# First projection with the activations held in TensorE: halves of 512 columns, x*C by tokens and then turned, and seven-product groups there and in the output projection

## Chip, cores and metric

The kernel runs on one core of a Trainium2 chip, as one program in one launch. The metric is the device time of that program in microseconds (us). The kernel before took 2130.61 us (median of 3 runs, 2130.58 to 2131.43).

## What is computed

A two-layer decoder trunk on 256 tokens (T) of width 2048 (D), all in float32. Only the first sub-layer is touched by the change:

```python
def short_conv_mixer(u, w_in, conv_w, w_out):
    proj = u @ w_in                                   # 256 x 2048 @ 2048 x 6144
    xin, gate_c, gate_b = jnp.split(proj, 3, axis=-1)
    v = gate_c * xin
    S = v.shape[1]
    vp = jnp.pad(v, ((0, 0), (CONV_WIDTH - 1, 0), (0, 0)))
    conv = sum(conv_w[k] * vp[:, k:k + S] for k in range(CONV_WIDTH))
    return (gate_b * conv) @ w_out                    # 256 x 2048 @ 2048 x 2048
...
h = h + rmsnorm(short_conv_mixer(rmsnorm(h, mix_pre_g[0]), ...), mix_post_g[0])
```

Behind it come a squared-ReLU MLP (2048 to 8192 and back), one shared K/V projection, a stick-breaking attention with its own query and output projections, and a second such MLP. The gain of each norm in front of a projection is multiplied into the operand; the 1/rms of a token may be applied later, since it is one number for each token.

## The kernel before

**Products.** A float32 product is made of three matmuls in the round format `fp32r`: each operand is split into a high part (ScalarE, a copy into `fp32r`: `split`, the `h...` tiles) and a low part (VectorE, raw minus high: `lower`, the `l...` tiles), and high·high, high·low and low·high are added up in PSUM. Weights come from memory in chunks of 512 KB (128 rows x 1024 columns, `chunk`), six raw pages deep.

**Two ways to hold operands.** In every projection but the first, a `Group` (16 chunks of K=128 rows, 1024 columns) holds the activations in TensorE (128 x 128: one K-chunk, one block of 128 tokens) and moves 512 weight columns past them; its output lies by tokens, in four PSUM banks `acc[b][c]` (token block b, column half c). Three such matmuls on one `acc` are one product (`product`, line 563). In the first projection (`convolution`) it is the other way round: a weight tile of 128 x 128 is held, and the 512 columns [high | low] of all 256 tokens move past it (`mms`, part 0), then the low weight tile with the 256 high columns (part 1), both recorded at line 437. The output lies by features, one bank for each of 48 column tiles, 16 K-chunks each. Six tiles are led in together (`lead`, `LEAD = 6`), K-chunk by K-chunk as the weights arrive; the other 42 follow one after another.

**Between the projections.** `combined` adds the two halves of the moved columns, `conv_tile` forms x*C, scales it by 1/rms squared, does the three taps along the tokens (shifts along the free dimension, so by features is the right layout), multiplies by B and 1/rms, and splits the result into the four tiles `y` that the output projection holds. `statistics` gets 1/rms of all tokens as a row by one matmul with ones.

**Seven products.** In most MLP groups some pairs of K-chunks (`seven`, `UP_SEVEN`, `DN_SEVEN`) do the 2 x 2 blocks (two K-chunks, two token blocks, two column halves) by seven products in place of eight, in the manner of Strassen and Winograd: VectorE adds and subtracts weight halves (four operations of 512 columns, `Group.seven`), the activation sums `XS` are formed ahead (`make_forms`), and four products of the seven go into banks of their own, `q5 q6 q1 q7`, which are the four banks that the group before has just left (`next_set`, `qset`). `combine` and `finals` add them into the outputs on VectorE. A group with seven-product pairs (`mixed`) starts with one ordinary pair, and its second pair is already a seven.

**What sets the order.** Every instruction is a task of `Plan`, which lists tasks engine by engine by estimated times and due times; side tasks of TensorE (transposes) are put into its queue where their inputs are expected. Each engine then runs its list strictly in that order. Pages are slots of fixed classes (`SLOTS`): `x4` 8, `c2` 12, `x8` 8.

Lines that the prediction uses: 390 ScalarE activations, 398 VectorE `tensor_tensor`, 405 VectorE `scalar_tensor_tensor`, 437 first projection's matmuls, 444 transposes (`tr`), 563 `product`.

Of the kernel before, what the change touches and what calls it, by code (L numbers as in the profile page):

```python
# [20 lines left out]
LEAD = 6  # L21
# [7 lines left out]
SLOTS = {"raw": 6, "rt": 2, "r2": 2, "hi": 6, "lo": 5, "x8": 8, "x4": 8, "c2": 12}  # L29
# [5 lines left out]
IN_N = [j * KD + i for i in range(KD) for j in range(3)]  # L35
IN_ORDER = [(k, n) for k in range(KD) for n in IN_N[:LEAD]] + [(k, n) for n in IN_N[LEAD:] for k in range(KD)]

# [49 lines left out]
class Plan:  # L87
# [77 lines left out]
    def place(self):  # L165
# [52 lines left out]
        while done < len(tasks):  # L218
# [39 lines left out]
            if e in ("SP", "POOL") and t.kb:  # L258
                issue = 0.06 if e == "SP" else 1.2
# [65 lines left out]
def trunk(ctx, tc, x, xT, vecs, rows, ws, hs, out):  # L325
# [202 lines left out]
    def form(XS, j, i, f):  # L528
        o = (i * 4 + FORM[f]) * P
        return XS[j].view([(o, o + P)], lambda t: t[:, i, FORM[f], :])  # L530

    def make_forms(XS, pairs, r0, r1, name):
# [14 lines left out]
        for j in pairs:  # L547
            XS[j] = page("x4", [P, 2, 4, P], F32R, f"{name}{j}")
            for r, f in ((r0, 0), (r1, 2)):
                src = r.col(j % 2 * 2 * P, (j % 2 + 1) * 2 * P).as3("p (k t) -> p k t", k=2)  # L550
                hi, lw = [
                    XS[j].view([((i * 4 + f) * P, (i * 4 + f + 2) * P)], lambda t, i=i, f=f: t[:, i, f : f + 2, :])
# [16 lines left out]
    class Group:  # L569


        def __init__(self, name, w, base, n, X, banks, evict, ks=1, gains=None, XS=None, sevens=(), seeds=None, qbanks=None, start=None):
            self.name, self.w, self.base, self.n, self.X, self.banks, self.evict = name, w, base, n, X, banks, evict
            self.ks, self.gains, self.XS, self.sevens, self.seeds, self.qbanks = ks, gains, XS, sevens, seeds, qbanks
            self.start = start
# [16 lines left out]
        def parts(self, i):  # L592
            if i not in self.split:
                gains = self.gains(i) if self.gains else None
                self.split[i] = chunk(self.w, self.base + i, f"{self.name}{i}", parts=len(gains) if gains else 1, gains=gains)
# [17 lines left out]
        def seven(self, j, last):  # L613
# [3 lines left out]
            if j in SUMS_BY_DMA:  # L617
                rs = raw_page(f"r{name}s")
                r1 = page("r2", [P, HALF], F32, f"r{name}b")
                twice = w[base + 1][:, HALF:].unsqueeze(1).to_broadcast([P, 2, HALF])  # L620
                load(rs.col().as3("p (a n) -> p a n", a=2), twice, own=(r0, rs))
# [99 lines left out]
        def whole(self):  # L721
# [193 lines left out]
    def convolution():  # L915
        rot = {"i": -1}

        def next_bank(name):
            rot["i"] += 1
            return bank(rot["i"] % 8, name)  # L920

        stores = [page("x4", [P, CW], F32, f"tmp{z}") for z in range(5)]

        def ring(places):
            at = {"i": -1}

            def take():
                at["i"] += 1
                return places[at["i"] % len(places)]
            return take  # L930

        quarter = [stores[z].col(q * T, (q + 1) * T) for z in range(4) for q in range(4)]
        vplaces = [stores[4].col(z * (T + 2), (z + 1) * (T + 2)) for z in range(2)]
        sums, halves, convs, vring = ring(quarter[:8]), ring(quarter[8:11]), ring(quarter[11:13]), ring(vplaces)
        rstd, rstd2 = quarter[13], quarter[14]
        u = [operand(f"u{c}") for c in range(4)]
        acc = page("c2", [P, 2 * T], F32, "sumsq")
        xpair, wsplit = {}, {}
        w = ws["in"]

        def load_x(q):
            if q < KD // 2:
                xpair[q] = page("c2", [P, 2 * T], F32, "x")
                load(xpair[q].col(), xT[:, q * 2 * T : (q + 1) * 2 * T])

        at_tile = {kn: i for i, kn in enumerate(IN_ORDER)}

        def mms(tiles):
            for part in range(2):
                for ps, k, n in tiles:  # L950
                    i = at_tile[k, n]
                    ci = i // CH
                    if ci not in wsplit:
                        wsplit[ci] = chunk(w, ci, f"in{ci}", parts=4 if ci < FIRST else 1)
                    o = i % CH * P
                    wv = wsplit[ci][part].col(o, o + P)
                    xs = u[k // 4].view([(at4(k % 4, 0), at4(k % 4, 0) + 4 * P)], lambda t, k=k: t[:, k % 4].rearrange("p a b t -> p (a b t)"))
                    xh = u[k // 4].view([(at4(k % 4, 0), at4(k % 4, 0) + 2 * P)], lambda t, k=k: t[:, k % 4, 0].rearrange("p b t -> p (b t)"))
                    if part == 0:
                        mm(ps.col(), wv, xs, 0.231, start=k == 0, stop=False)  # L960
                    else:
                        mm(ps.col(0, T), wv, xh, 0.12, start=False, stop=k == KD - 1)

        def combined(ps):
            b = halves()
            act(b, ps.view([(0, 2 * T)], lambda t: t[:, T : 2 * T]), AF.Copy, soon=2.0)
            s = sums()
            tt(s, ps.col(0, T), b, ALU.add, soon=3.0)
            return s

        def enter(k):
            xp, gain = xpair[k // 2].col(k % 2 * T, (k % 2 + 1) * T).as3("p (b t) -> p b t", b=NB), g(G_MIX0, k)
            act(both(u, k, 0), xp, AF.Copy, scale=gain)
            stt(both(u, k, 1), xp, gain, both(u, k, 0), ALU.mult, ALU.subtract)
            if k % 2:
                if k == 1:
                    act(acc.col(), xpair[0].col(), AF.Square, soon=20.0)
                else:
                    sq = page("c2", [P, 2 * T], F32, "sq")
                    act(sq.col(), xpair[k // 2].col(), AF.Square, soon=20.0)  # L980
                    tt(acc.col(), acc.col(), sq.col(), ALU.add, soon=25.0)

        y = [None] * 4
        state = {"scale": False}

        def statistics():
            tt(acc.col(0, T), acc.col(0, T), acc.col(T, 2 * T), ALU.add)
            ps = bank(LEAD - 1, "ms")
            mm(ps.col(0, T), ones.col(), acc.col(0, T), 0.44)
            act(rstd, ps.col(0, T), AF.Sqrt, bias=eps.col(), scale=1.0 / D)  # L990
            recip(rstd)
            tt(rstd2, rstd, rstd, ALU.mult)
            state["scale"] = True

        for o in (0, T + 2):
            v = stores[4].col(o, o + 2)
            plan.task("DVE", 0.1, lambda v=v: nc.vector.memset(v.w(), 0.0), [], [v])

        def conv_tile(i, sx, sc, sb):
            tt(sx, sx, sc, ALU.mult)  # L1000
            v = vring()
            tt(sub(v, 2, T + 2), sx, rstd2, ALU.mult)
            c = convs()
            act(c, sub(v, 2, T + 2), AF.Copy, scale=g(G_C2, i))
# [442 lines left out]
```

## Time and profile before

| | |
|---|---|
| median of three runs | 2130.61 us |
| the profiled execution, its time | 2130.27 us |
| its span | 2128.5 us |
| granted TensorE clock | 0.999 |
| TensorE first matmul | 5.88 us |
| first projection on TensorE | 5.88 to 276.40 us |
| output projection on TensorE | 276.40 to 363.96 us |
| VectorE busy in these two | 194.17 and 45.43 us |

Times inside the profile count from the start of the span. A row of matmuls starts when its first one starts; rows overlap, since a matmul's recorded time includes its way through the array, so the pace of TensorE is read from start to start, not from the mean duration.

### The profile page before, as it was taken

The numbers are of one execution on the slowest core, as the hardware profiler recorded it, in microseconds if no ns is written. First come the engines' busy times: TensorE is split into PE (matmuls) and PEld (weight loads), VectorE is DVE, ScalarE is ACT, GpSimd is POOL, SyncE is SP. The second block draws the span as 40 slices with busy tenths as digits, with TensorE's granted clock in tenths as the row PEclk, the third lists the DMA queues.
The fourth block names the chain that finished last, engine by engine and source line by source line (L and its number), as shares of the span: only waits on it lengthen the run. The fifth ranks groups of instructions, "written<-read, shape, count | busy, mean of one in ns | idle before, by whom it ended". The sixth has DMA issues, their size and how long they took to land.

```text
span 2128.5 us, 28143 instructions
## 1 busy us (share of the span) xinstructions
PE 2111.5 (99%) x9900; PEld 1764.5 (83%) x9900; DVE 1770.7 (83%) x2456; ACT 1307.8 (61%) x1830; POOL 1.0 (0%) x7
## 2 busy tenths in 40 slices
PE   8999999999999999999999999999999999999998
PEld 7888888888888888888888888888888888888886
DVE  7766656899999999999656777558999999999995
ACT  7444445766576576567657776547755765675673
POOL 0000000000000000000000000000000000000000
PEclk9999999999999999999999999999999999999999
DMA  8655576556656755667665455656566566656673
GB/s 288 190 190 189 188 252 199 185 187 218 204 186 198 228 182 195 208 211 248 215 205 168 158 168 170 232 180 220 172 203 227 180 198 208 207 181 208 197 267 127
DMA packets 118653, 427.63 MB, mean 201 GB/s; under 512 B 13168, under 2 KB 13296, under 8 KB 118512
## 3 DMA queue, kind: packets, MB, share of 16 engines
q1 hardware_dynamic: 118368, 425.77, 60.9%
q8 instruction: 77, 1.26, 0.2%
q14 instruction: 64, 0.52, 0.1%
q10 hardware_dynamic: 144, 0.07, 0.0%
HBM read 417.40 MB, written 8.39 MB: 200 GB/s over the span
## 4 chain that ended last, share of the span: by engine, by line
PE 98%; DVE 1%; ACT 1%; issue 0%; DMA 0%; DVEq 0%; ACTq 0%
PE acc L563 69%; PE q L563 12%; PE acc L437 11%; PE tr L444 2%; PE lead L437 2%; PE o L1264 0%; PE z L1214 0%; DVE hh L405 0%; DVE lv L405 0%; ACT hid L390 0%; DVE lu L398 0%; DMA gv<-vecs 0%; ACT hu L390 0%; PE ex L1244 0%; PE o L1265 0%
## 5 line engine op out<-in xcount | busy, mean ns | idle before, releaser
L563 PE MATMUL acc<-hu,u 128*128 128x512 f32 x1544 | 493.1, 392 | 0.0
L563 PE MATMUL acc<-hd,hid 128*128 128x512 f32 x1376 | 438.1, 391 | 0.0
L563 PEld LDWEIGHTS acc<-hu,u 128*128 128x128 f32 x1544 | 289.7, 188 | 59.6 <-DVE u L405 0.8
L563 PEld LDWEIGHTS acc<-hd,hid 128*128 128x128 f32 x1376 | 258.5, 188 | 52.9
L563 PE MATMUL acc<-lu,u 128*128 128x512 f32 x772 | 300.9, 390 | 0.0
L563 PE MATMUL acc<-ld,hid 128*128 128x512 f32 x688 | 268.2, 390 | 0.0
L390 ACT ACTIVATE hu<-ru 128x1024 fp32r<-128x1024 f32 x172 | 180.2, 1061 | 103.4 <-PE acc L563 86.0
L398 DVE TENSOR_TENSOR lu<-ru,hu 128x1024 fp32r<-128x1024 f32 x172 | 208.1, 1221 | 27.8 <-PE acc L563 21.3
L398 DVE TENSOR_TENSOR ld<-rd,hd 128x1024 fp32r<-128x1024 f32 x144 | 174.0, 1220 | 24.3 <-PE acc L563 23.9
L390 ACT ACTIVATE hd<-rd 128x1024 fp32r<-128x1024 f32 x144 | 148.3, 1054 | 55.9 <-PE acc L563 40.0
L398 DVE TENSOR_TENSOR lin<-rin,hin 128x1024 fp32r<-128x1024 f32 (+1 forms) x102 | 117.6, 1161 | 69.1 <-PE acc L437 62.5
L390 ACT ACTIVATE hin<-rin 128x1024 fp32r<-128x1024 f32 (+1 forms) x102 | 102.0, 1007 | 111.9 <-PE acc L437 73.3
L563 PEld LDWEIGHTS acc<-lu,u 128*128 128x128 f32 x772 | 145.1, 188 | 28.9
L437 PE MATMUL acc<-u,hin 128*128 128x512 f32 x672 | 168.5, 393 | 0.0
L563 PEld LDWEIGHTS acc<-ld,hid 128*128 128x128 f32 x688 | 129.3, 188 | 26.1
L437 PEld LDWEIGHTS acc<-u,hin 128*128 128x128 f32 x672 | 121.1, 189 | 21.5
L563 PE MATMUL q<-hd,hs 128*128 128x512 f32 x336 | 121.8, 390 | 0.0
L437 PEld LDWEIGHTS acc<-u,lin 128*128 128x128 f32 x672 | 91.7, 191 | 6.5
L437 PE MATMUL acc<-u,lin 128*128 128x256 f32 x672 | 93.7, 283 | 0.0
L563 PE MATMUL q<-hu,us 128*128 128x512 f32 x252 | 91.9, 391 | 1.4 <-ACT hid L390 1.4
L563 PE MATMUL acc<-hk,u 128*128 128x512 f32 x256 | 87.1, 400 | 0.0
L563 PE MATMUL acc<-hv,u 128*128 128x512 f32 x256 | 82.8, 395 | 0.1
(1340 smaller groups left out, 4087.2 us busy)
## 6 DMA issues: line engine op xcount, KB each, us to landing
ru<-w_up SPq DMA_DIRECT2D x172, 512.0 KB, 4.3
rd<-w_dn SPq DMA_DIRECT2D x144, 512.0 KB, 4.3
rin<-w_in SPq DMA_DIRECT2D x94, 512.0 KB, 3.5
ro<-w_out SPq DMA_DIRECT2D x32, 512.0 KB, 4.2
rv<-w_v SPq DMA_DIRECT2D x32, 512.0 KB, 3.7
rk<-w_k SPq DMA_DIRECT2D x32, 512.0 KB, 3.7
rq<-w_q SPq DMA_DIRECT2D x32, 512.0 KB, 3.5
rwo<-w_wo SPq DMA_DIRECT2D x32, 512.0 KB, 3.4
```

Of the source, the lines that this page charges most:

```text
L390: nc.scalar.activation(out_.w(), in_.r(), func, scale=val(scale), **more)
L398: "DVE", dve(width(out_)), lambda: nc.vector.tensor_tensor(out_.w(), a.r(), b.r(), op=op),
L437: lambda: nc.tensor.matmul(out_.w(), lhsT.w(), rhs.w(), start=start, stop=stop, skip_group_check=skip),
L444: nc.tensor.matmul(to.w(), src.r(), ident.tile[:], is_transpose=True, start=j == 0, stop=True, skip_group_check=True)
L563: nc.tensor.matmul(ps.w(), a.w(), w.w(), start=first and j == 0, stop=last and j == 2, skip_group_check=skip)
```

## The change

The first projection becomes six ordinary `Group`s. The columns of `w_in` are put in another order on the host, so that the twelve halves of 512 columns stand as xin, C, B, xin, C, B, ... for four runs f = 0..3 of 512 features; each group takes two halves. The outputs now lie by tokens, so 1/rms is one number for each partition: `statistics` loads x once more by tokens (8 pages of 256 KB) and sums squares on ScalarE; the matmul with ones goes. When a half is done, VectorE forms x*C*(1/rms)^2 by tokens (`evict`, kind 1), TensorE turns it (`turned`: 8 transposes of 128 x 128 into the two banks just left), ScalarE copies it out and the taps are done by features as before, 256 columns at a time (`convolve`); B likewise is scaled on ScalarE, turned and multiplied in (`gate`). In all 64 transposes are added.

Groups 1 to 5 (`IN_SEVEN`) and the first of the two output groups (`OUT_SEVEN`) get three seven-product pairs each; the activation sums come from `make_forms_of`. The two output groups are now run one by one. `Plan` counts 0.45 us for each DMA that SyncE issues, where it counted 0.06; behind the output projection the order of TensorE and of SyncE's loads is the same, row for row.

```diff
@@ seven()
+    if stage == "in":
+        return IN_SEVEN if j else ()
+    if stage == "out":
+        return OUT_SEVEN if j == 0 else ()
...
+IN_SEVEN = (0, 1, 2)
+OUT_SEVEN = (0, 1, 2)
@@ trunk()
+    def make_forms_of(XS, j, r, name):
+
+        a11, a21, a12, a22 = (r.col(z * P, (z + 1) * P) for z in range(4))
+        tt(a22, a21, a22, ALU.subtract)
+        tt(a21, a21, a11, ALU.subtract)
+        tt(a11, a11, a22, ALU.subtract)
+        tt(a12, a12, a11, ALU.subtract)
+        to = page("x4", [P, 2, 4, P], F32R, f"{name}{j}")
+        XS[j] = to, {"s2": 0, "s3": 1, "s4": 2, "s1": 3}
...
+        act(hi, r.col(), AF.Copy)
+        tt(lw, r.col(), hi, ALU.subtract)
@@ Group.whole()
             for i in range(self.n):
+                if self.on:
+                    self.on(i)
                 for b in range(NB):
                     self.unit(b, i, i == self.n - 1)
+            if self.before_out:
+                self.before_out()
@@ convolution() and what is before it
-    def convolution():
-        rot = {"i": -1}
...
+        def statistics():
+            for b in range(NB):
+                for c in range(4):
+                    xs = page("c2", [P, 512], F32, "xs")
+                    load(xs.col(), rows512(x, b, c), soon=20.0)
+                    act(dump.col(), xs.col(), AF.Square, accum=ss[b][c], soon=25.0)
...
+        def turned(banks, c, srcs):
+
+            pss = [bank(banks[b][c], "tr") for b in range(NB)]
+            for z in range(2):
+                transposes(
+                    [pss[z].col((m * NB + e) * P, (m * NB + e + 1) * P) for m in range(2) for e in range(NB)],
+                    [sub(srcs[e], (2 * z + m) * P, (2 * z + m + 1) * P) for m in range(2) for e in range(NB)],
+                )
+            return pss
...
+                if add is not None and kind:
+                    tt(add, ps, add, op, soon=1.5)
+                    ps = add
+                if kind == 0:
...
+                elif kind == 1:
+                    v = xin[f][b]
+                    stt(v, v, r2[b], ps, ALU.mult, ALU.mult, soon=1.5)
+                    if b == NB - 1:
+                        convolve(f, banks, c)
+                else:
+                    to = ps if add is not None else page("c2", [P, 512], F32, "gate").col()
+                    act(to, ps, AF.Copy, scale=r1[b], soon=1.5)
+                    waiting.setdefault(f, []).append(to)
+                    if b == NB - 1:
+                        gate(f, banks, c, waiting.pop(f))
...
+        for gi in range(6):
+            banks, qb = next_set()
+            groups.append(Group(
+                f"in{gi}", ws["in"], gi * KD, KD, u, banks, evict(gi, banks), XS=uS, sevens=seven("in", 0, 0, gi), qbanks=qb
+            ))
@@ the output projection
-    outs = two_groups("o", ws["out"], y, mix0)
+    outs = two_groups("out", ws["out"], y, mix0, yS)
     outs[0].start = mix0.prepare
-    run(outs, leave=True)
+    run(outs[:1])
+    run(outs[1:], leave=True)
```

**TensorE at the start.** Before, the first six tiles of K-chunk 0: `hin0` and `lin0` are the high and low weights of chunk 0, `u0` the activations of K-chunks 0 to 3, `lead` the six banks.

```order
L437 MATMUL lead_183<-u0_175,hin0_179 128x512
L437 MATMUL lead_189<-u0_175,hin0_179 128x512
L437 MATMUL lead_192<-u0_175,hin0_179 128x512
L437 MATMUL lead_195<-u0_175,hin0_179 128x512
L437 MATMUL lead_199<-u0_175,hin0_179 128x512
L437 MATMUL lead_203<-u0_175,hin0_179 128x512
L437 MATMUL lead_183<-u0_175,lin0_187 128x256
```

Now, with `hin00` and `lin00` the first chunk of group 0 and `acc00` to `acc11` its four banks:

```order
L581 MATMUL acc00_201<-hin00_184,u0_176 128x512
L581 MATMUL acc00_201<-lin00_191,u0_176 128x512
L581 MATMUL acc01_213<-hin00_184,u0_176 128x512
L581 MATMUL acc01_213<-lin00_191,u0_176 128x512
L581 MATMUL acc10_224<-hin00_184,u0_176 128x512
L581 MATMUL acc10_224<-lin00_191,u0_176 128x512
```

The second matmul of the program now needs the low half of the weights; before, the seventh did.

**TensorE where one piece of output ends and the next begins.** Before, from one column tile to the next (`acc_1436`, then `acc_1488`), in the middle of the first projection:

```order
L437 MATMUL acc_1436<-u2_340,hin47_1330 128x512 x4
L437 MATMUL acc_1436<-u3_414,hin47_1330 128x512 x4
L437 MATMUL acc_1436<-u2_340,lin47_1366 128x256 x4
L437 MATMUL acc_1436<-u3_414,lin47_1366 128x256 x4
L437 MATMUL acc_1488<-u0_175,hin48_1356 128x512 x4
L437 MATMUL acc_1488<-u1_248,hin48_1356 128x512 x4
```

Now, from group 2 (halves C and B of f = 1) to group 3: `hin36` and `hin37` are the first two chunks of group 3, `xin` is x*C by tokens, `q2` and `q3` are B of token blocks 0 and 1, `tr_1396` to `tr_1424` the four banks of group 2, and `q5_1456`, `q6_1463` lie in the first and the last of these banks.

```order
L581 MATMUL acc11_1389<-hin36_1298,u1_290 128x512
L447 MATMUL tr_1396<-ident_70,xin_1052 128x128
L447 MATMUL tr_1401<-ident_70,xin_1052 128x128
L581 MATMUL acc00_1371<-hin37_1305,u1_290 128x512
L447 MATMUL tr_1415<-ident_70,q2_1303 128x128
L447 MATMUL tr_1415<-ident_70,q3_1331 128x128
L447 MATMUL tr_1424<-ident_70,q3_1331 128x128
L581 MATMUL acc01_1377<-hin37_1305,u1_290 128x512
L581 MATMUL q5_1456<-hin300_1358,us0_256 128x512
L581 MATMUL q6_1463<-hin300_1358,us0_256 128x512
```

(One row stands for each run of alike ones: the transposes are eight of `xin` and eight of `q2`, `q3`, and there are four products of `hin36` ahead of them, one of `hin37` between them, three behind them.) The eight transposes of x*C now stand behind four products of the next group, and the eight of B one product later; `q5` and `q6` need the banks that these transposes filled, once ScalarE has emptied them.

**VectorE at the same place.** Before, between two column tiles (`tmp` tiles hold xin, C, B and the taps by features, `lin23`, `lin24` low weights):

```order
L398 TENSOR_TENSOR tmp0_568<-acc_676,tmp2_554 128x256
L398 TENSOR_TENSOR y4_683<-tmp1_592,y4_683 128x256
L398 TENSOR_TENSOR tmp0_568<-tmp0_568,tmp3_622 128x256 x2
L398 TENSOR_TENSOR lin23_765<-rin23_612,hin23_725 128x1024
L398 TENSOR_TENSOR y4_683<-tmp0_568,y4_683 128x256
L398 TENSOR_TENSOR lin24_790<-rin24_629,hin24_755 128x1024
```

Now, at the end of group 2 (`acc00_990` to `acc11_1011` are its banks, `q0` to `q3` the sums of `combine`, `stat11` and `stat12` (1/rms)^2 of the two token blocks, `rin30b`, `rin30c` weight sums for group 3's first seven):

```order
L401 TENSOR_TENSOR lin37_1343<-rin37_1251,hin37_1305 128x1024
L401 TENSOR_TENSOR rin30c_1338<-rin30c_1338,rin30a_1279 128x512
L401 TENSOR_TENSOR rin30b_1291<-rin30b_1291,rin30a_1279 128x512
L401 TENSOR_TENSOR q0_1270<-acc00_990,q0_1270 128x512
L401 TENSOR_TENSOR q2_1303<-acc01_998,q2_1303 128x512
L401 TENSOR_TENSOR q1_1289<-acc10_1003,q1_1289 128x512
L408 SCALAR_TENSOR_TENSOR xin_1047<-xin_1047,stat11_84,q0_1270 128x512
L408 SCALAR_TENSOR_TENSOR xin_1052<-xin_1052,stat12_85,q1_1289 128x512
L401 TENSOR_TENSOR q3_1331<-acc11_1011,q3_1331 128x512
L401 TENSOR_TENSOR lin300_1393<-rin30c_1338,hin300_1358 128x1024
```

Six operations in a row empty the four banks and form x*C, where before one addition of 256 columns emptied a bank and its bank was not asked for until seven tiles later.

More of the change, by code (lines that the diff above doesn't have):

```diff
@@ L20 @@
 EPS = 1e-6
-LEAD = 6
 CH = 8
@@ L258, in place @@
             if e in ("SP", "POOL") and t.kb:
-                issue = 0.06 if e == "SP" else 1.2
+                issue = 0.45 if e == "SP" else 1.2
                 avail[e] = s + issue
@@ L528, in form @@
     def form(XS, j, i, f):
-        o = (i * 4 + FORM[f]) * P
-        return XS[j].view([(o, o + P)], lambda t: t[:, i, FORM[f], :])
+        tile_, at = XS[j]
+        o = (i * 4 + at[f]) * P
+        return tile_.view([(o, o + P)], lambda t: t[:, i, at[f], :])
+    def make_forms_of(XS, j, r, name):
[6 more added lines that the diff above has]
+        XS[j] = to, {"s2": 0, "s3": 1, "s4": 2, "s1": 3}
+        hi, lw = [to.view([(i * 4 * P, (i + 1) * 4 * P)], lambda t, i=i: t[:, i].rearrange("p f t -> p (f t)")) for i in range(2)]
+        act(hi, r.col(), AF.Copy)
+        tt(lw, r.col(), hi, ALU.subtract)
     def make_forms(XS, pairs, r0, r1, name):
@@ L547, in make_forms @@
         for j in pairs:
-            XS[j] = page("x4", [P, 2, 4, P], F32R, f"{name}{j}")
+            to = page("x4", [P, 2, 4, P], F32R, f"{name}{j}")
+            XS[j] = to, FORM
             for r, f in ((r0, 0), (r1, 2)):
@@ L911, in squares @@
                 recip(r)
-    def convolution():
-        rot = {"i": -1}
[L918 to L1004, printed above, removed]
-            stt(c, sub(v, 1, T + 1), g(G_C1, i), c, ALU.mult, ALU.add)
-            stt(c, sub(v, 0, T), g(G_C0, i), c, ALU.mult, ALU.add)
-            tt(sb, sb, rstd, ALU.mult)
-            tt(sb, sb, c, ALU.mult)
-            if y[i // 4] is None:
-                y[i // 4] = operand("y4")
-            src = sb.as3("p (b t) -> p b t", b=NB)
-            act(both(y, i, 0), src, AF.Copy)
-            tt(both(y, i, 1), src, both(y, i, 0), ALU.subtract)
-        for q in range(3):
-            load_x(q)
-        pss = [next_bank("lead") for _ in range(LEAD)]
-        for k in range(KD):
-            if k % 2 == 0:
-                load_x(k // 2 + 3)
-            if k == 0:
-                enter(0)
-                enter(1)
-            elif k % 2 and k + 2 < KD:
-                enter(k + 1)
-                enter(k + 2)
-            mms([(ps, k, n) for ps, n in zip(pss, IN_N[:LEAD])])
-        lead = [combined(ps) for ps in pss]
-        for i in range(LEAD // 3, KD):
-            new = []
-            for j in range(3):
-                ps = next_bank("acc")
-                for k in range(0, KD, CH):
-                    mms([(ps, k + m, IN_N[3 * i + j]) for m in range(CH)])
-                if not state["scale"]:
-                    statistics()
-                new.append(combined(ps))
-                if lead and j == 1:
-                    conv_tile(LEAD // 3 - len(lead) // 3, *lead[:3])
-                    del lead[:3]
-            conv_tile(i, *new)
-        return y
@@ L1061, in mlp @@
+    y, yS = convolution()
     def mlp(i, before, after):
@@ L1135, in sublayer, with evict @@
     def sublayer(norms, j):
-        return lambda b, c, ps: norms.post(b, 2 * j + c, ps)
+        def evict(b, c, ps, add=None, op=None):
+            if add is not None:
+                tt(add, ps, add, op, soon=2.0)
+            norms.post(b, 2 * j + c, ps if add is None else add)
+        return evict
     mix0 = Norms("mix0", B_POST0, x, hs, gain=G_MLP0, sevens=UP_SEVEN)
@@ L1416 @@
     arrays["rows"] = np.ascontiguousarray(np.broadcast_to(np.stack(rows)[:, None, :], (len(rows), P, D)))
-    arrays["w_in"] = tiled(a["a_w_in"][0], IN_ORDER)
-    arrays["w_out"] = banded(a["a_w_out"][0])
+    w_in = a["a_w_in"][0].reshape(D, 3, 4, HALF).transpose(0, 2, 1, 3).reshape(D, 3 * D)
+    arrays["w_in"] = banded(w_in, sevens=[seven("in", 0, 0, j) for j in range(6)])
+    arrays["w_out"] = banded(a["a_w_out"][0], sevens=[seven("out", 0, 0, j) for j in range(2)])
     arrays["w_wo"] = banded(a["b_w_o"][0])
```

118 lines of the change are left out of this document (98 added, 20 removed).

## The prediction

> **What bounds the kernel now.** I read the page's busy shares first, then its chain of waits.
>
> ```profile
> PE 2111.5 (99%) x9900; PEld 1764.5 (83%) x9900; DVE 1770.7 (83%) x2456; ACT 1307.8 (61%) x1830; POOL 1.0 (0%) x7
> PE 98%; DVE 1%; ACT 1%; issue 0%; DMA 0%; DVEq 0%; ACTq 0%
> ```
>
> 98% of the chain is TensorE, so a change counts by what it adds to or takes from TensorE's queue, and by the waits it puts there. Next the busy time in chosen stretches: the start, the first projection, the output projection, and one quarter of the first MLP (columns: stretch and length, busy us and count of PE, PEld, DVE, ACT, POOL, then granted clock, DMA share, GB/s).
>
> ```profile
> 10.00:20.00 10.00, 10.00 (x58) 8.72 (x58) 9.82 (x15) 9.74 (x19) 0.00 (x0) 1.00 1.03 409
> 20.00:40.00 20.00, 20.00 (x117) 17.57 (x116) 15.51 (x21) 13.00 (x17) 0.00 (x0) 1.00 0.87 307
> 5.88:276.40 270.52, 270.52 (x1538) 238.06 (x1539) 194.17 (x287) 142.11 (x208) 0.00 (x0) 1.00 0.65 216
> 276.40:363.96 87.56, 87.56 (x390) 72.52 (x389) 45.43 (x52) 37.92 (x50) 0.00 (x0) 1.00 0.64 201
> 443.94:612.12 168.18, 168.18 (x760) 139.59 (x759) 162.32 (x209) 103.88 (x129) 0.00 (x0) 1.00 0.61 199
> ```
>
> TensorE has no hole in either stretch that the change touches, and the clock is full. The MLP quarter shows that groups with seven-product pairs run with TensorE full while VectorE is busy 162.3 of 168.2 us: the case that the first projection moves towards.
>
> **The pace of TensorE.** From the timeline, the end of the first projection; from the chain in order of time, a stretch of the MLP.
>
> ```profile
> 273.61 2.00 PE L437 MATMUL acc<-u,hin 128*128 128x512 f32 x8
> 275.45 1.11 PE L437 MATMUL acc<-u,lin 128*128 128x256 f32 x8
> 276.40 0.40 PE L563 MATMUL acc<-ho,y 128*128 128x512 f32 x1
> ...
> 443.94 12.25 PE acc L563 x54
> 456.19 0.44 PE tr L444 x4
> ...
> 458.45 0.87 PE tr L444 x8
> ```
>
> Start to start, eight weight tiles take 276.40 - 273.61 = 2.79 us, 0.3494 for each (eight matmuls of 512 columns 1.84, so 0.230 each; eight of 256 columns 0.95). With activations held, 54 matmuls take 12.25 us: 0.2269 each, 0.6806 a product. A transpose costs 0.87/8 = 0.109.
>
> **Part by part, on TensorE.**
>
> *The operand held.* Before: 16 x 48 = 768 weight tiles x 0.3494 = 268.3 us. As ordinary groups it is 6 groups x 16 chunks x 4 = 384 products x 0.6806 = 261.4. The moved columns are the same (768 x 768, and 384 x 1536); only the pace differs: -6.9 us. [...]
>
> *Seven products.* Five groups with three pairs and one output group with three: 18 products go, 18 x 0.6806 = -12.2 us. The order confirms the count: 1107 matmuls of 512 columns in the first projection (369 products) and 375 in the output projection.
>
> *Turning.* 8 places (x*C and B for four f) x 8 transposes = 64 x 0.109 = +7.0 us. Against that speaks the duration of one in the view of the tile `tr`:
>
> ```profile
> L444 PE MATMUL tr<-ident,q x224: 269/273/273, 456.0 to 2036.5; 128*128 128x128 f32 x112
> ```
>
> 273 ns is its way through the array, of which 8 in a row pay little: 0.87 us for all. [...]
>
> *The start.* Before and now at the start, TensorE, VectorE and ScalarE:
>
> ```profile
> 5.88 2.93 PE L437 MATMUL lead<-u,hin 128*128 128x512 f32 x6 [5.88 <-ACT hin L390]
> 8.61 1.39 PE L437 MATMUL lead<-u,lin 128*128 128x256 f32 x6
> 9.83 1.55 PE L437 MATMUL lead<-u,hin 128*128 128x512 f32 x6
> 5.96 0.75 DVE L398 TENSOR_TENSOR lin<-rin,hin 128x256 fp32r<-128x256 f32 x2
> 6.99 1.43 DVE L398 TENSOR_TENSOR lin<-rin,hin 128x256 fp32r<-128x256 f32 x4 [0.28 <-ACT hin L390]
> 6.56 1.32 ACT L390 ACTIVATE hin<-rin 128x256 fp32r<-128x256 f32 x4
> ```
>
> The first twelve matmuls took 9.83 - 5.88 = 3.95 us, where six tiles at pace take 2.10: 1.85 lost. Now the second matmul needs two low quarters of chunk 0 (VectorE, done 6.7 as before), and the fourth needs the other two quarters: high at about 7.3 (from 6.56, two of four in 0.66), low about 7.9. Then `acc01` starts its low product at about 8.1, ends 8.6, and two more products end at 10.0: chunk 0 ends 1.4 us later than 5.88 + 4 x 0.68 = 8.6. So -0.4 us. If the quarters hide, the loss is 0.3; one chunk late again makes it 2 x 1.4. Chunk 1 is there by then (before, its four low quarters had room from 6.99 on). Later chunks: a pair of chunks needs on VectorE 2 x 1.14 for lows, 2 x 0.40 for `u`, some 1.6 for the sums of one pair: 4.7 us in 5.4 of TensorE. Loads: 16 chunks of 512 KB and 16 pages of 256 KB (x, once by features and once by tokens) are 12.6 MB in some 44 us, 286 GB/s; the rows above show 409 and 307 at the start. SyncE's queue now has eight loads of x between chunks 9 and 16; I give that no cost, and it has 0.7 us (below) for each chunk that comes late if that cover is gone. The statistics matmul goes:
>
> ```profile
> 46.92 0.59 PE L437 MATMUL ms<-sumsq,ones 128*128 128x256 f32 x2
> 47.16 1.05 PE L437 MATMUL acc<-u,hin 128*128 128x512 f32 x3
> ```
>
> -0.24 us. (5.88 + 1.85 + 268.3 + 0.24 = 276.3: the sum meets the 276.40 of before.)
>
> *VectorE, in total.* Durations of one (x count | busy, mean ns | idle before):
>
> ```profile
> L398 DVE TENSOR_TENSOR lin<-rin,hin 128x1024 fp32r<-128x1024 f32 x94 | 114.8, 1224 | 68.8 <-PE acc L437 62.5 <-ACT hin L390 2.2 <-PE lead L437 2.2
> L398 DVE TENSOR_TENSOR q<-q,q 128x512 f32<-128x512 f32 x112 | 76.4, 682 | 0.0
> L405 DVE SCALAR_TENSOR_TENSOR hh<-mg,stat,hh 128x512 f32<-128x512 f32 x32 | 22.6, 747 | 0.3
> L405 DVE SCALAR_TENSOR_TENSOR tmp<-tmp,gv,tmp 128x256 f32<-128x256 f32 x32 | 15.2, 481 | 0.5
> L390 ACT ACTIVATE tk<-acc,stat 128x512 f32<-128x512 f32 x16 | 10.9, 681 | 0.3 <-PE acc L563 0.2
> ```
>
> In groups 1 to 5 the order has 94 of 1024 columns (1.22), 125 of 512 (0.68), 4 x 0.75, 24 taps x 0.48 and 12 of 128 columns (about 0.3): 218 us, for 305 products and 48 transposes, 212.8 us of TensorE. But neighbours overlap by 0.08 us each:
>
> ```profile
> 609.13 3.50 DVE L398 TENSOR_TENSOR lu<-ru,hu 128x1024 fp32r<-128x1024 f32 x3
> ```
>
> three take 3.50, not 3.66. 259 operations less 0.08 each: 197.6 us, 93% of TensorE's time, where the MLP quarter had 96.5% without a wait. VectorE moves near its limit, and stays hidden.
>
> *The ends of groups.* The new waits are here. Group 2 to 3 is the tightest. With T = 0 the end of its last product, `acc11`: VectorE, if prompt, takes `q0`, `q2`, `q1`, the two x*C and `q3` from T = -1.8 on and is done at 2.2 (four x 0.68, two x 0.75, less the overlap), x*C at 1.5. TensorE reaches the eight transposes of x*C at 4 x 0.68 = 2.7 and those of B at 4.3; B is scaled on ScalarE (0.68) by 3.0. So about 1 us is in hand at both. `q6` comes at 7.9 and needs the last bank emptied by ScalarE; two copies of x*C, three taps and two of B behind it end at about 7.6. Little in hand there, and a miss is small. The nearest row for a miss is the one place in the first MLP where an ordinary group gives way to a mixed one:
>
> ```profile
> 420.52 0.50 PE L563 MATMUL q<-hu,us 128*128 128x512 f32 x1 [0.69 <-ACT hid L390]
> ```
>
> 0.69 us. There are seven such ends (into groups 1 to 5, and into and out of the first output group), so 0 to 4.8 us. I take 0.5 in all, near the lower end, since the mixed groups of the MLP quarter show none. Behind the output projection TensorE's order is unchanged, and I give it no cost; its own waits there come to a few tenths each.
>
> **Sum.** -6.9 - 12.2 + 7.0 - 0.4 - 0.2 + 0.5 = -12.2 us. From the profiled execution's 2130.27 (span 2128.5 and 1.8 around it), that is 2118.1; the median of three runs lies 0.3 above that execution, so 2118.4 us. The first MLP matmul, at 363.96 before, should come at about 351.8.
>
> **Rivals.**
>
> *Every group end waits* (14%). Seven times 0.69 in place of 0.5: 2118.4 + 4.3 = 2122.7. For it: ScalarE's taps stand ahead of the copies of B. Against it: the room worked out above.
>
> *The pace belongs to the stage, not to the operand held* (4%). If matmuls of 512 columns go at 0.230 in this stretch whatever is held, 1107 x 0.0035 = 3.9 us less is won: 2122.3. Against it: the output projection behind it, with activations held, needs 87.56 us for 384 products and four transposes, 0.227 a matmul. [...]
>
> *VectorE becomes the bound* (4%). If its operations did not overlap here, 218 against 212.8 us: 5.6 us more, 2124.0. Against it: the MLP quarter.
>
> *VectorE is late at the turns, and the kernel is slower* (3%). TensorE's queue is strict: where transposes wait, the products behind them wait too. The cover is 2.7 us. If VectorE came to `q0` only one low chunk after the group's end (T = 1.2), x*C would be ready at 1.2 + 5 operations, about 3.3, + 0.2 = 4.7, 2.0 late; eight turns x 2.0 = 16 us: 2134. It decides from 12.2/8 = 1.5 us a turn. Against it: VectorE can work ahead by five low pages, and is 93% loaded.
>
> *Transposes cost their duration* (1%). 64 x (0.273 - 0.109) = 10.5 us more: 2128.9, no change that can be told. Against it: the rows of eight. [...]
>
> That the change does not do what it says is excluded by the order, which has the 54 matmuls less.
>
> **Numbers.** My forecast, 2118.4 within 2 us, has 72%; the five rivals 26%, and 2% stay for something that I do not see. The range holds the forecast with its bounds below (start loss 0.3: -1.1; no waits: -0.5; 0.4 for the spread of runs: 2116.4) and reaches above to the waits at every end, 2122.8. 0.2% is 4.3 us, about what a measurement of this kernel can tell from no change: faster is below 2126.3. That is the forecast and the first three rivals, 94%; same 2%; slower 4%.
>
> **What would show it.** Right: first MLP matmul near 351.8; first output matmul at 5.9 + 1.4 + 251.2 + 48 x 0.109 = 263.7 or up to 0.5 later; `product` at 0.227 start to start; turns of 0.87; no idle row before `q5` or `q6` over 0.4 us; VectorE busy about 93% there. Wrong: a row of transposes with idle before it that names VectorE, in each group (late VectorE); rows of `q` with idle naming ScalarE (group ends); 0.230 a matmul; or a stretch behind 352 that is longer than the 1764.5 us it has now, which no term of mine allows.

## The result, and the profile after

The changed kernel takes 2118.73 us, median of four runs (2117.7 to 2119.44), against 2130.8 (2130.58 to 2131.43) for the kernel before on the same chip: a ratio of 0.9942, 95% interval 0.9925 to 0.996, 12 us less. The profiled execution has a span of 2116.9 us. One run of a later kernel, the one with every transpose twice, took 2346.4 us at a granted clock of 0.85 and is left out of that kernel's figures.

The page of the changed kernel, its busy shares and the shares of its chain:

```profile
PE 2099.6 (99%) x9524; PEld 1739.5 (82%) x9524; DVE 1838.0 (87%) x2536; ACT 1338.2 (63%) x1863; POOL 1.0 (0%) x7
PE 97%; DVE 2%; ACT 1%; issue 0%; DMA 0%; DVEq 0%; ACTq 0%
```

TensorE still carries the time, with 376 matmuls fewer and 12 us less. VectorE went from 1770.7 to 1838.0 us. The busy time in the stretches that answer to those of before (start of the first projection to the first output matmul, and from there to the first MLP matmul):

```profile
10.00:20.00 10.00, 10.00 (x45) 8.29 (x44) 9.88 (x19) 9.99 (x20) 0.00 (x0) 1.00 1.03 407
20.00:40.00 20.00, 20.00 (x90) 16.57 (x89) 16.77 (x30) 17.43 (x34) 0.00 (x0) 1.00 1.03 400
6.27:265.18 258.91, 258.83 (x1155) 213.98 (x1156) 239.75 (x334) 162.46 (x222) 0.00 (x0) 1.00 0.65 226
54.58:265.18 210.60, 210.52 (x952) 174.35 (x951) 203.65 (x267) 127.93 (x157) 0.00 (x0) 1.00 0.61 204
265.18:352.47 87.29, 87.29 (x397) 72.43 (x396) 66.01 (x87) 48.47 (x67) 0.00 (x0) 1.00 0.65 222
```

The first projection shrank from 270.52 to 258.91 us. VectorE fills 239.75 of it (92.6%) where it filled 194.17 of 270.52, and TensorE is still full. The row from 54.58 on is groups 1 to 5 alone, from the first transposes: there VectorE fills 203.65 of 210.60 us, 96.7%. At 10 to 40 us the loads run at 407 and 400 GB/s, and TensorE waits for none of them, SyncE's eight loads of x between the chunks included. The output projection went from 87.56 to 87.29: three products less, sixteen transposes more. The first MLP matmul stands at 352.47, where it stood at 363.96, so 11.49 of the 11.6 us are won by then; behind it lie 2116.9 - 352.47 = 1764.43 us, before 2128.5 - 363.96 = 1764.54.

TensorE's waits in the whole changed kernel (total us, times, longest):

```profile
PE acc L581 <- ACT hin L393: 6.3, 1, 6.3
PE q L581 <- ACT hid L393: 1.4, 2, 0.7
PE tr L447 <- DVE mg L401: 1.0, 2, 0.5
PE acc L581 <- DVE lv L408: 0.6, 2, 0.3
```

The first is the start; the other three the kernel before had as well. No row names a group end of the first projection. The chain in order of time, at group 0 and then at the end of group 2:

```profile
6.27 48.47 PE acc L581 x204
54.74 0.87 PE tr L447 x8
...
139.50 0.87 PE tr L447 x8
140.37 0.70 PE acc L581 x3
141.07 0.87 PE tr L447 x8
...
144.03 2.04 PE q L581 x9
```

At group 2's end everything follows at pace: 0.87 for eight transposes, and `q5` and `q6` start in their place behind 144.03. But group 0 has lost time. In the timeline its 204 matmuls begin at 6.27 and the transposes behind them at 54.58; that is 48.31 us (the chain's 48.47 takes in the recorded end of the last one), and at 0.2269 they would take 46.29: 2.02 lost. The timeline of TensorE shows where:

```profile
6.27 0.79 PE L581 MATMUL acc<-hin,u 128*128 128x512 f32 x1 [6.27 <-ACT hin L393]
6.86 0.78 PE L581 MATMUL acc<-lin,u 128*128 128x512 f32 x1
7.44 1.05 PE L581 MATMUL acc<-hin,u 128*128 128x512 f32 x2
8.30 0.63 PE L581 MATMUL acc<-lin,u 128*128 128x512 f32 x1
8.72 1.05 PE L581 MATMUL acc<-hin,u 128*128 128x512 f32 x2
9.58 0.63 PE L581 MATMUL acc<-lin,u 128*128 128x512 f32 x1
10.00 0.74 PE L581 MATMUL acc<-hin,u 128*128 128x512 f32 x2
10.58 0.40 PE L581 MATMUL acc<-lin,u 128*128 128x512 f32 x1
10.81 0.62 PE L581 MATMUL acc<-hin,u 128*128 128x512 f32 x2
```

From 8.30 to 8.72 is one matmul, 0.42 us; from 10.58 to 10.81 is one too, 0.23. No idle time stands ahead of any but the first. Nor do the low weights explain it: VectorE has the first two quarters at 6.80 and the other two at 7.71, and the low matmuls that want them start at 6.86 and 8.30. So only the second matmul can have waited for them. A slow pace, and not a wait for operands, takes up most of the start, although the profile reads a granted clock of 1.00 there.

### The profile page after: what moved, and what is told of

The parts are those of the page before. It is cut to its first block, busy times and chain, and to the rows that moved or that the text cites. A ratio compares the mean times of both kernels' runs of the same rounds, so it can differ in the third digit from the quotient of the medians.

```text
span 2116.9 us, 27566 instructions
## 1 busy us (share of the span) xinstructions
PE 2099.6 (99%) x9524; PEld 1739.5 (82%) x9524; DVE 1838.0 (87%) x2536; ACT 1338.2 (63%) x1863; POOL 1.0 (0%) x7
## 4 chain that ended last, share of the span: by engine, by line
PE 97%; DVE 2%; ACT 1%; issue 0%; DMA 0%; DVEq 0%; ACTq 0%
PE acc L581 79%; PE q L581 15%; PE tr L447 2%; DVE hh L408 0%; PE o L1299 0%; PE z L1249 0%; DVE lu L401 0%; DVE lin L401 0%; DVE lv L408 0%; ACT hid L393 0%; DMA gv<-vecs 0%; ACT hu L393 0%; PE ex L1279 0%; PE o L1300 0%; PE z L1250 0%
## 5 line engine op out<-in xcount | busy, mean ns | idle before, releaser
L401 DVE TENSOR_TENSOR lu<-ru,hu 128x1024 fp32r<-128x1024 f32 x172 | 207.9, 1221 | 28.3 <-PE acc L581 18.8
L581 PE MATMUL acc<-hin,u 128*128 128x512 f32 x588 | 186.6, 393 | 6.3 <-ACT hin L393 6.3
L581 PEld LDWEIGHTS acc<-hin,u 128*128 128x128 f32 x588 | 111.3, 189 | 29.2 <-ACT hin L393 6.3
L581 PE MATMUL acc<-lin,u 128*128 128x512 f32 x294 | 115.3, 392 | 0.0
L401 DVE TENSOR_TENSOR q<-q,q 128x512 f32<-128x512 f32 x136 | 92.8, 682 | 0.2
L401 DVE TENSOR_TENSOR lin<-rin,hin 128x1024 fp32r<-128x1024 f32 (+1 forms) x72 | 80.0, 1131 | 7.4 <-PE acc L581 4.6
L581 PE MATMUL acc<-hq,u 128*128 128x512 f32 x256 | 81.6, 393 | 0.0
```

The source lines that it names most:

```text
L401: "DVE", dve(width(out_)), lambda: nc.vector.tensor_tensor(out_.w(), a.r(), b.r(), op=op),
L581: nc.tensor.matmul(ps.w(), a.w(), w.w(), start=first and j == 0, stop=last and j == 2, skip_group_check=skip)
```

## The experiments

The theory: the change is worth what TensorE's queue loses, the operand held (-6.9), the products (-12.2) and the transposes (+7.0), and nothing else changes much, since VectorE stays hidden. The rivals: the transposes cost their duration, or VectorE is the limit at the group ends or in total. Each kernel below is an edit of the changed one, unless it says otherwise; all were timed in five rounds beside the kernel before. They ran in three sets, on three chips, each with its own runs of the kernel before; a difference from the change compares medians across sets. The kernel before took 2130.51 to 2130.8 us in all of them.

**No products saved.** This leaves the form of the first projection and its turns, and takes all eighteen products back.

```
-IN_SEVEN = (0, 1, 2)
-OUT_SEVEN = (0, 1, 2)
+IN_SEVEN = ()
+OUT_SEVEN = ()
```

> The change without its seven-product pairs (first projection and output projection all in ordinary products). My theory: the 18 products come back, 18 x 0.6806 = 12.2 us, and about 0.3 us of waits in group 3, where VectorE was full, goes: 2118.7 + 11.9 = 2130.6, so the same as before within 0.5 us: what holding the activations wins (6.9) the 64 transposes eat (7.0). Rival, the pace belongs to the stage: had the operand held won nothing, 2118.7 would have to come from elsewhere and this run would stand near 2130.8 + 6.9 = 2137. Rival, the sevens hide a cost in VectorE: then more than 1 us of the 12.2 is not lost, and this is below 2129.6.

2130.81 us (2129.95 to 2131.56), ratio 1.0002 (0.9993 to 1.001), as expected. The new form alone wins nothing: what the held activations save, the turns and the start take back. Its first output matmul is at 275.33 against 276.40, and its first MLP matmul at 364.67 against 363.96. It also shows the pace by itself: from the first transposes at 55.06 to 275.33 are 220.27 us for 948 matmuls and 48 transposes, and less 48 x 0.109 that is 0.2268 a matmul, so 261.3 us for all 1152, where the 768 weight tiles of before took 268.3 by their rows.

**Only the output projection's products taken back.**

```
-OUT_SEVEN = (0, 1, 2)
+OUT_SEVEN = ()
```

> The change with the output projection's three seven-product pairs taken away, those of the first projection kept. My theory: three products, 3 x 0.6806 = +2.0 us: 2120.8. Rival, the first output group waits for its sums or for pages (the sums of pair 2 and six pages for the norm are wanted there): then less than 1 us is lost: below 2119.8.

2120.98 us (2120.41 to 2121.11), ratio 0.9956 (0.9944 to 0.9968). Against the run without any, fifteen products are worth 9.8 us (15 x 0.6806 = 10.2); the last three then 2.25 (2.04). In the traces the output projection takes 89.34 us in both runs and 87.29 in the change, 2.05 less.

**Every transpose twice.** The eight transposes of each turn run a second time into the same banks, to the same values.

```
-                transposes(
+                t = transposes(
...
+                t.fn = lambda once=t.fn: (once(), once())
```

> Every turn of x*C and of B in the first projection is done twice into the same banks (64 more transposes, output unchanged); the order of all else stays. My theory: 64 x 0.109 = +7.0 us: 2125.7. Rival, a transpose costs its recorded duration: 64 x 0.273 = +17.5: 2136. Rival, transposes stand in waits of TensorE and cost little: under +3.

2125.07 us (2124.6 to 2125.93), ratio 0.9976 (0.9967 to 0.9985): 6.3 more for 64 transposes, 0.10 each. In the trace, from the first transposes at 53.90 to the first output matmul at 269.74 are 215.84 us against 210.60, so 5.24 for 48, 0.109 each. Their duration did not change, as the view of the tile `tr` shows (min, median and max in ns):

```profile
L447 PE MATMUL tr<-ident,xin x64: 270/273/273, 53.9 to 274.1; 128*128 128x128 f32 x64
```

64 x 0.273 would be 17.5. The rival of the duration falls.

**A fourth pair in the first projection.** Five products less, 3.4 us of TensorE, for more sums on VectorE.

```
-IN_SEVEN = (0, 1, 2)
+IN_SEVEN = (0, 1, 2, 4)
```

> The change with four seven-product pairs in each of groups 1 to 5 (pair 4 as well), three in the output group as before. TensorE: 5 products fewer, -3.4 us. VectorE: each more pair costs it some 4.2 us (four sums of 512 columns, 0.60 each, 1.2 more columns to lower, 1.75), so a group has about 44 us of VectorE in 42 of TensorE. My theory, VectorE is at its limit: the 3.4 is not won, and the excess of some 2 us a group shows as waits of TensorE for low weights: 2120 to 2126. Rival, VectorE stays hidden as the MLP's groups of four suggest (they have 96.5% of it): 2115.3.

2133.2 us (2132.05 to 2134.35), ratio 1.0013 (1.0004 to 1.0021), 14.5 more than the change and beyond what I expected. TensorE's new waits, and busy time and granted clock in groups 1 to 5 and around two of the waits (columns as above, the granted clock third from the end):

```profile
PE acc L581 <- DVE lin L401: 5.9, 11, 1.0
PE q L581 <- DVE lin L401: 5.4, 7, 1.7
```

```profile
55.14:280.89 225.75, 214.41 (x937) 171.28 (x936) 223.09 (x296) 135.44 (x167) 0.00 (x0) 0.99 0.56 185
150.00:180.00 30.00, 27.11 (x113) 20.50 (x111) 29.97 (x46) 16.92 (x23) 0.00 (x0) 1.00 0.49 159
180.00:188.00 8.00, 6.98 (x22) 5.31 (x23) 8.00 (x9) 4.68 (x5) 0.00 (x0) 0.79 0.66 238
```

From the first transposes to the first output matmul VectorE is busy 223.09 of 225.75 us, 98.8%: the stretch is now as long as VectorE's work, and TensorE waits 11.3 us for low weights. So a fourth pair in all five groups is more than VectorE carries here, and the total of VectorE, not only its promptness, is what the next step would meet. (Whether a fourth pair in one or two groups would fit, no run tells.)

A wait cost more here than its row counts:

```profile
180.59 0.62 PE L581 MATMUL acc<-hin,u 128*128 128x512 f32 x2
181.99 0.50 PE L581 MATMUL acc<-lin,u 128*128 128x512 f32 x1 [0.77 <-DVE lin L401]
182.32 1.02 PE L581 MATMUL acc<-hin,u 128*128 128x512 f32 x2
```

Two matmuls from 180.59 on would let the third start at 181.04; it starts at 181.99, 0.95 later, and the next comes 0.33 behind it instead of 0.23: 1.05 us where the row says 0.77. Worked out so from start to start, the 18 waits cost 16.6 us. Behind the last line the matmuls are 0.42 apart until about 186, and the clock in the 8 us around it is 0.79: 1.6 us of loss on top. Group 0 was done 0.6 later than in the change's profile. These are 18.8 of the 19.1 us to be explained (15.7 more of span, with 3.4 us less work).

**VectorE late at every group end.** Twelve idle operations of 128 columns (2.5 us) stand ahead of the first operation that empties a bank, at each of the six ends.

```
+                    if gi not in held:
+                        held.add(gi)
...
+                        for _ in range(12):
+                            nc.vector.tensor_tensor(ones.tile[:], ones.tile[:], ones.tile[:], op=ALU.mult)
```

> At the end of each of the six groups of the first projection, VectorE does twelve idle multiplications of 128 columns (about 0.2 each, 2.5 us) ahead of its first operation on the group's banks; the order of everything else stays. In the change's trace the turns have 0.35 to 1.7 us in hand (x*C of group 2 ready at 138.1, turned from 139.3; group 3's ready at 184.1, turned from 184.4). Theory: each end is late by 2.5 less what it has in hand: about 0.8 + 1.2 + 1.4 + 2.1 + 1.6 + 1.7 = 8.7 us, 2127.4, and no more than the 14.8 us of work added, 2133.5, if VectorE's own limit shows too. Rival, TensorE's queue has more cover than I read: under +3, 2121.7.

2137.42 us (2134.42 to 2139.53), ratio 1.003 (1.0018 to 1.0042): beyond both expectations. Its waits, and then the timeline of TensorE at the end of group 2:

```profile
PE tr L447 <- DVE xin L408: 7.3, 6, 2.5
...
PE tr L447 <- ACT q L393: 2.4, 2, 1.4
...
PE q L581 <- DVE xin L401: 0.3, 1, 0.3
```

```profile
143.83 0.48 PE L447 MATMUL tr<-ident,xin 128*128 128x128 f32 x1 [2.46 <-DVE xin L408]
144.50 1.76 PE L447 MATMUL tr<-ident,xin 128*128 128x128 f32 x7 [0.19 <-DVE xin L408]
145.90 0.78 PE L581 MATMUL acc<-hin,u 128*128 128x512 f32 x1
...
147.33 1.91 PE L447 MATMUL tr<-ident,q 128*128 128x128 f32 x8
...
149.89 0.84 PE L581 MATMUL acc<-hin,u 128*128 128x512 f32 x2
```

The waits sum to 10.0 us. After the one of 2.46 the matmuls are 0.42 to 0.43 apart (0.57 and 0.58 for the first behind a row of transposes) and the transposes about 0.2, twice the usual 0.23 and 0.109, until about 150. The granted clock says the same:

```profile
144.00:147.00 3.00, 2.81 (x11) 2.33 (x12) 3.00 (x4) 2.14 (x5) 0.00 (x0) 0.50 0.02 5
```

This happened after the ends of groups 2, 3 and 5, where TensorE had waited 2.46, 2.06 and 1.74 us at one place, and not after the 1.03 and 1.40 of groups 1 and 4. At half clock from 143.8 to 150, from 195.5 to 201.4 and, less a wait of 0.33, from 286.1 to 290.2, half of some 15.9 us is lost, 8 us. With the 10.0 that makes 18 of the 20.5 us by which the first MLP matmul is late in this profiled execution (372.94). 2.5 stay; some of that is again what a wait costs beyond its row (the 1.03, 1.40 and 0.30, which no half pace follows, took 1.16, 1.60 and 0.57 from start to start). How far the half pace follows may differ from execution to execution: the mean granted clock is 0.995 in the three that took 2138.66 to 2139.53 us and 0.997 to 0.998 in the three that took 2134.42 to 2136.18.

**VectorE a little late.** Five idle operations, about 1.05 us.

```
-                        for _ in range(12):
+                        for _ in range(5):
```

> The changed kernel with five idle VectorE operations (about 1.05 us) instead of twelve (2.5 us) ahead of the first evicting operation at each of the six group ends. With twelve TensorE stood for 10.0 us in all, and after the three waits of 1.7 to 2.5 us it ran at half pace for 4 to 6 us more; after those of 1.0 and 1.4 it did not. Theory (the free time at the turns is 0.35 to 1.35 us, and half pace comes only after the long waits): 1.05 us late cost at most what is over the free time, some 0.3 to 2.5 us over the six ends, no stretch with a granted clock of 0.50, 2119.0 to 2121.2. Rival (VectorE has nothing in hand, each delay shows whole): 6 x 1.05 = 6.3, 2125.0.

2123.64 us (2123.18 to 2124.75), ratio 0.9969 (0.9957 to 0.998): 4.9 more, near the rival's 6.3 and not in my range. No stretch of the first projection has a clock below 1.00. The waits that it adds are short:

```profile
PE tr L447 <- DVE xin L408: 0.9, 2, 0.6
PE q L581 <- DVE lin L401: 0.8, 1, 0.8
PE tr L447 <- ACT q L393: 0.8, 1, 0.8
...
PE q L581 <- ACT bt L393: 0.3, 1, 0.3
PE q L581 <- DVE xin L401: 0.3, 1, 0.3
```

Nearly half lies outside the turns' rows (`tr`). They sum to 3.1, and to 4.4 from start to start. The first MLP matmul comes at 356.43, 4.0 later than in the change, though the first transposes came 0.84 earlier (53.74 against 54.58), so 4.8 were lost between them. Another 0.7 lies behind the first MLP matmul, and not in the work: from the last VectorE operation to the end of the span are 4.16 us here and 3.36 in the change, which no edit touches. What holds: the free time at the turns is real, but VectorE, full within the group, does not make up 1.05 us before the next thing that is asked of it.

**Idle matmuls ahead of the start.** If the slow pace of the start (0.42 us a matmul) is TensorE's own, work ahead of it may end it. First 44 matmuls of ones by ones with 128 columns, into a bank that nobody reads, ahead of the first one of the changed kernel:

```
+        for _ in range(44):
+            nc.tensor.matmul(wb.tile[:, :P], ones_r.tile[:], ones_r.tile[:], start=True, stop=True)
```

> The change with 44 idle matmuls (ones by ones, 128 columns) on TensorE from about 1.6 us on, while it waits for its first operands; all else as in the change. In the change's trace the first matmuls go at 0.43 us start to start until 10 us, and chunk 0 ends at 11.0 where I had 10.0. Theory A, TensorE is slow because it was idle before: now chunk 0 goes at 0.227 a matmul but for the waits for VectorE's low quarters that I worked out (to about 8.1), and ends at 10.0 to 10.4: -0.6 to -1.0 us, 2117.9. Theory B, as I predicted, VectorE's low quarters set the pace there: no change, 2118.7 within 0.3, and the first rows still 0.43 apart.

2123.15 us (2122.6 to 2123.62), ratio 0.9966 (0.9954 to 0.9978), worse than the change. Its timeline, with VectorE's last low quarters of chunk 0:

```profile
1.38 9.65 PE L486 MATMUL warm<-ones_r 128*128 128x128 f32 x44 [1.38 <-DVE eps L463]
6.51 0.76 DVE L401 TENSOR_TENSOR lin<-rin,hin 128x256 fp32r<-128x256 f32 x2 [0.16 <-ACT hin L393]
10.82 0.73 PE L589 MATMUL acc<-hin,u 128*128 128x512 f32 x1
...
15.20 0.63 PE L589 MATMUL acc<-lin,u 128*128 128x512 f32 x1
15.62 0.71 PE L589 MATMUL acc<-hin,u 128*128 128x512 f32 x2
```

The short matmuls took 9.4 us, 0.21 each, and held the real ones up; and behind them the real ones still ran 0.42 apart for 4.8 us, until about 15.6. That rules out theory B, since all low quarters of chunk 0 were there at 7.27, 3.5 us ahead of the first real matmul. It does not show theory A, since work ahead did not end the slow pace. The same 44 ahead of the kernel before:

> The kernel before, with the same 44 idle matmuls ahead of its first one. Its first six matmuls stood 0.45 us apart (2.73 for six). If idleness made them slow (theory A): six at 0.23, then low quarters as they come, -1.0 to -1.5 us, 2129.5. If VectorE or ScalarE set the pace (theory B): no change, 2130.8 within 0.3.

2135.08 us (2134.29 to 2135.62), ratio 1.0021 (1.0013 to 1.003): the first real matmul at 10.82 as well, and so slower too; its first six then take 2.61 us (10.82 to 13.43) where they took 2.73.

**Full matmuls ahead of the start.** Eleven of 512 columns, started at 1.38; the first real one comes at 5.99, where it came at 6.27 in the change:

```
+        for _ in range(11):
+            nc.tensor.matmul(wb.tile[:, : 4 * P], ones_r.tile[:], ones_r.tile[:].unsqueeze(1).to_broadcast([P, 4, P]), start=True, stop=True)
```

> The changed kernel with eleven idle matmuls of 512 columns (ones by ones, into bank 0, never read) ahead of its first one, in the time in which TensorE waits for the first operand anyway: 11 x 0.43 = 4.7 us from about 1.4. With 44 of 128 columns the earlier try filled 9.4 us and ended no slow pace. Theory that the slow pace of the start (about 9 matmuls of 512 columns at 0.43 us where 0.23 comes later) is TensorE's own and is ended by some 4 us of full matmuls: the real ones run at 0.23 from the first or soon after, gain between 0.6 (the operands come late then) and 1.8 (9 x 0.2), 2116.9 to 2118.1. Rival, that the pace hangs on the time since launch or on the operands and not on TensorE's work: no gain, 2118.7 within 0.4, and the real matmuls still 0.43 apart until about 10.7.

2117.16 us (2116.94 to 2117.45), ratio 0.9938 (0.9924 to 0.9951).

```profile
1.38 4.78 PE L486 MATMUL warm<-ones_r 128*128 128x512 f32 x11 [1.38 <-DVE eps L463]
5.99 0.40 PE L589 MATMUL acc<-hin,u 128*128 128x512 f32 x1
6.46 0.50 PE L589 MATMUL acc<-lin,u 128*128 128x512 f32 x1
6.79 0.64 PE L589 MATMUL acc<-hin,u 128*128 128x512 f32 x2
7.38 0.50 PE L589 MATMUL acc<-lin,u 128*128 128x512 f32 x1
7.72 0.63 PE L589 MATMUL acc<-hin,u 128*128 128x512 f32 x2
```

From 7.72 on the real matmuls run 0.23 apart (two to the next row at 8.18); those before are 0.3 to 0.47 apart, from which cause no run tells. The first output matmul comes at 263.49 instead of 265.18, the span is 2115.1 instead of 2116.9. From the first real matmul to the first transposes are 46.88 us, 0.59 over pace. In the change and in the six experiments that leave its start alone it is 47.89 to 49.28 us, 1.60 to 2.99 over pace, with the same work. If all of that is half pace, it lasted twice as long, some 3 to 6 us; that is an estimate. So the start is a matter of the execution too, but all seven lost more than this one. This is the fastest kernel here: 1.6 us under the change by the medians, their ranges do not meet, though the two were not timed side by side and their intervals against the kernel before overlap. The same in the kernel before:

> The kernel before with the same eleven idle matmuls of 512 columns (into bank 7) ahead of its first one. Theory: its first six matmuls run at 0.23 instead of 0.455, so 1.35 us at most are won, 2129.5 to 2130.4. Rival (pace not set by TensorE's earlier work): 2130.8 within 0.4.

2129.2 us (2128.96 to 2129.93), ratio 0.9994 (0.9985 to 1.0003), just under what I expected: its first six matmuls take 1.7 us instead of 2.73, and its first MLP matmul comes at 362.77 instead of 363.96. The median is 1.5 us lower than before's 2130.71 on that chip, but the interval does not exclude no change. The traces of both kernels agree: with eleven matmuls of 512 columns ahead the pace of the start was faster, 1.71 us for six of 512 columns against 2.73, and 0.59 over pace against 1.60 to 2.99. Why 4.6 us of these did it and 9.4 us of the short ones did not, no run tells.

## Why the prediction came out right, step by step

The forecast was 2118.4 us, the time is 2118.73. The sum and the large terms hold; the start was off by 1.0. The profiled executions differ by 11.6 where the sum had 12.2. That the median is only 0.3 off is partly chance: it lies 0.1 above its profiled execution, where I had added 0.3.

- *Seven products*, -12.2: the two runs that take them back give 9.8 + 2.25 = 12.05 by the medians.
- *Turning*, +7.0: doubled, 6.3 by the medians, and 0.109 each in the trace.
- *The operand held*, -6.9: the run without sevens has 0.2268 a matmul over 948 of them, where the prediction had 0.2269. As a sum, that run's first output matmul is 1.07 earlier than before; by the terms it should be 6.9 + 0.2 earlier, 5.2 later by its 48 transposes, and 1.0 later by its own start (2.99 lost from 5.78 on, against 1.85 from 5.88): 0.9.
- *The start*, -0.4, was mis-sized: here it cost 0.6. The step that failed is "two more products end at 10.0: chunk 0 ends 1.4 us later than 5.88 + 4 x 0.68". It counted the low quarters of VectorE and then 0.68 for a product. But the quarters held up the second matmul at most, and the matmuls there go at about half pace, 0.42 us each; the twelfth begins at 10.81. The loss is 2.02, and 0.39 for a first matmul at 6.27 instead of 5.88, so 2.41 against 1.85 before. The rows of before had it: six matmuls of 512 columns in 8.61 - 5.88 = 2.73, which is 0.455 each. I read the 1.85 off them as a sum and did not ask what made it. The run with full idle matmuls shows that it is TensorE's pace for the most part: with them 0.59 of the 2.02 is left. How much is lost there differed between executions, 1.60 to 2.99 us. Over the seven with this start the term comes out between -0.3 and +1.2; of the kernel before there is one trace without idle matmuls.
- *The ends of groups*, +0.5: there is no wait in the list, but the 210.60 us of groups 1 to 5 are 0.5 over 903 x 0.2269 + 48 x 0.109 = 210.1, as forecast. Without sevens the same stretch meets its sum (220.27 against 220.3), so the 0.5 goes with the sevens; no row says where it lies.
- *VectorE, in total*, 93% in groups 1 to 5, was too low: it is 96.7% there, 203.65 us where I had 197.6, with 267 operations where I counted 259. Hidden it stays, as said, but with 7 us of room in five groups and not 15. That this is the edge is shown by the fourth pair: one more of its kind in each group, and TensorE waits.
- *Behind 352*: 1764.43 against 1764.5.

The sum with the start so sized, at the first MLP matmul, is -11.2, or -11.5 with the terms not rounded; measured are -11.49 (352.47 - 363.96). Of the signs named ahead one failed by the same step: the first output matmul was to come at 263.7 or up to 0.5 later, and came at 265.18. The first MLP matmul came at 352.47, where I had 351.8.

Two slips in the working touch no term of the sum: the output projection has 384 matmuls, not 384 products, and 0.230 is 0.0031 above 0.2269, not 0.0035, so that rival stands at 2121.8.

The rivals. That every group end waits, that the pace belongs to the stage and that transposes cost their duration are each refuted by a row above. VectorE as the bound did not come about, though at 96.7% it is near. "VectorE is late at the turns" did not come about either, but its price was too low in two ways: I had 1.5 us a turn as the point at which the gain is gone; a delay of 1.05 us at six ends took 4.9 of it, and one of 2.5 took all, with idle time of 10.0 us and half pace behind it.

## What to carry to other kernels

Where TensorE carries the chain, count what leaves and enters its queue at the pace of start to start, in the form in which it runs (held operand, columns), not by durations (a transpose here: 0.109 us of the queue, 0.273 recorded); that gave the large terms within 0.7 us each. When a second engine is nearly full beside it (VectorE 92.6% in the first projection here), take its share over the stretch where the work is densest (96.7% in groups 1 to 5), and ask for the next increment as well: a saving of 3.4 us of TensorE that asked for a little more of VectorE turned 12 us of gain into a loss. A row at an odd pace, such as 0.455 where 0.23 is usual, is worth asking about before its sum is taken over.

## What the runs showed of the hardware that I had not expected

- TensorE ran at half pace at the start of the kernel (0.42 to 0.43 us for a matmul of 512 columns, later 0.23), while the granted clock of the profile reads 1.00. It lasted some 3 to 6 us by the estimate from the loss of 1.60 to 2.99 us, which differed between executions with the same work.
- In one profiled execution the half pace came back behind single waits of 1.74, 2.06 and 2.46 us in the middle, there with a granted clock of 0.50, for 4 to 6 us; behind waits of 1.03 and 1.40 us it did not. In the run with a fourth pair it came behind five waits of 0.38 to 1.06 us between 170.50 and 181.99 (the last two 0.70 and 0.77), and did not come behind five of 0.18 to 1.66 us between 78.54 and 88.18. So a wait at the end of a group cost up to some 3 us beside its own length (an estimate, half of the 6.2 us from 143.8 to 150), and in these two runs its length alone did not tell whether it would.
- A wait of TensorE ahead of a matmul of 512 columns cost 0.27 to 0.45 us more, from start to start, than the idle time in its row (18 waits of the run with a fourth pair; the one shown 1.05 against 0.77).
- 44 matmuls of 128 columns, 9.4 us without a hole, did not end the half pace; eleven of 512 columns, 4.6 us, nearly did: the real ones behind them were 0.30 to 0.47 us apart until 7.72 and 0.23 from there on.
